# Moving two weight pools to the other side of SBUF, keeping the row-sum reciprocals on chip, and reusing the FFN's operand tiles in the down stage

## The chip, the cores and the metric

The kernel runs on one core of one Trainium2 chip. The metric is the device time of one execution in microseconds; lower is better. Engines are named as in the profile: PE is TensorE (PEld its weight loads), DVE VectorE, ACT ScalarE, POOL GpSimd, SP the engine that issues most of the transfers (SPq its queue).

## What is computed

One layer of a decoder trunk on 1024 tokens plus 16 meta tokens, width 1024, in fp32. Cut to what matters here:

```python
u = rmsnorm(h, attn_norm_w)
# 4 delta-rule heads -> o_gdn (512 columns); 8 softmax heads of width 64 -> o_fox (512 columns)
p = softmax(where(causal, scores, MASK)); o_fox = p @ v
h = h + concat([o_gdn, o_fox]) @ w_out
u2 = rmsnorm(h, ffn_norm_w)
h = h + (silu(u2 @ w_gate) * (u2 @ w_up)) @ w_down      # hidden width 2816
return rmsnorm(h, final_norm_w)[:, 16:]
```

## The kernel before

**Precision.** Every large product is made of three fp32r matmuls: a `split` (L156 to L159) makes a high part by a cast on ACT and a low part by a subtraction on DVE, and high times high, high times low and low times high are accumulated.

**Order of work.** The stages follow each other: input projection, delta rule, attention, out-projection, gate and up stage of the FFN, down stage. On PE the order is the program's, by hand (`manual_schedule`); in attention it comes from a small planner (`PeOrder`) with estimated due times. The other engines' and the queues' orders come from the scheduler of the framework, which puts an instruction where its own timeline says that it will be ready; once emitted, each engine and each queue runs in order.

**Attention** (to L1037). For each of the 8 heads the unnormalised output goes to a DRAM tensor `o_d` in two halves (high and low value parts), and the reciprocals of the row sums are transposed on PE (`prr`, L1034), copied out of PSUM and stored in a DRAM tensor `ri_d` by `att_sums`.

**Out-projection.** The delta-rule half is `wout_gdn` (L1062): 16 units of 12 matmuls, of which six (`RES`) run after attention. Then the softmax half runs over eight token tiles in the order 0, 4, 1, 5, 2, 3, 6, 7. For one tile, `prep` (L1129) loads both halves of `o_d` (`of`) and the reciprocals, spread over the partitions, from `ri_d` (`rb`, one buffer, two transfers, L1137), adds and multiplies on POOL (L1139, L1140), splits into `oh` and `ol` and loads the running sum (`hst`). `out_fox` (L1146) makes 12 matmuls for each half of the columns, adds `hst` on DVE (L1152) and, after the second half, normalises: squares on ACT, a power on POOL (L204), one long DVE instruction (`xn`, L1045). `u_blocks` (L1161) transposes `xn` on PE (`u2t`, 8 transposes) and builds the operands of seven block products `p1` to `p7` (a Strassen-like scheme with 7 instead of 8 products): two of them for tiles 0 to 3, five for tiles 4 to 7. `prep` runs two tiles ahead, `u_blocks` two behind. The tiles of this stage lie in pool `wo1`, on the left side of SBUF over space that the delta-rule half still uses.

**Gate and up stage.** For each of 11 column blocks `j`, `ffn_in` runs 14 units of 12 matmuls (products p1, p6, p2, p7, p5, p4, p3, each for gate and up). `w_ops` loads and combines the weights and splits them into 8 pairs of buffers that rotate; raw weights have four rotating buffers, also used by `down_sums`, which combines the down weights on POOL and stores them in `wt_d`. `act_sums` stores the combined activations in `ao_d`. For `j` = 0 three units (`p1` gate, `p1` up, `p2` gate) have their weights early.

**Down stage.** For each of seven products, `down_ops` (L1347) loads activations and weights in three chunks of 4, 4 and 3 blocks into a new pool `f2`, which is opened after the pools of the stage before are closed, and splits them; 12 matmuls per block and token group follow (L1380).

Of the kernel before, what the change touches and what calls it, by code (L numbers as in the profile page):

```python
# [15 lines left out]
P = 128  # L16
# [21 lines left out]
RES = 6  # L38
WARM = 24
# [55 lines left out]
def tile_hymba_layer(ctx, tc, x, meta, attn_norm_w, w_in, conv_w, a_log, dt_bias, gdn_norm_w,  # L95
# [40 lines left out]
    nc.gpsimd.memset(mhalf, -0.5)  # L136

# [12 lines left out]
    ri_d = dram.tile([FH, S], F32, name="ri_d")  # L150
# [943 lines left out]
    atc.close()  # L1094
# [11 lines left out]
    uoc, pfc, woc, f1c = ExitStack(), ExitStack(), ExitStack(), ExitStack()  # L1106
    uop = uoc.enter_context(tc.tile_pool(name="uop", bufs=1, side="right", reuse_waits="tile"))
    uo = {p: tuple(uop.tile([P, 4, H], F32R, name=f"u{c}_{p}") for c in "hl") for p in ORD}
    pfp = pfc.enter_context(tc.tile_pool(name="pf", bufs=1, side="right", reuse_waits="tile"))
    wo = woc.enter_context(tc.tile_pool(name="wo1", bufs=1, reuse_waits="tile"))  # L1110
    nwb2 = wo.tile([P, D], F32, name="nwb2")
    xns = {}
    turn = {}

    def wo_tile(tag, shape, bufs, nm, dt=F32):
        turn[tag] = turn.get(tag, -1) + 1
        return wo.tile(shape, dt, tag=f"{tag}_{turn[tag] % bufs}", name=f"{tag}_{nm}")

    sq = [P, 4, P]
    for tag, shape, dt in ([(f"br{g}_{i}", sq, F32) for g in range(2) for i in range(2)]  # L1120
                           + [(f"xn2_{i}", [P, D], F32) for i in range(2)] + [(f"ub{i}_0", sq, F32) for i in range(3)]
                           + [(f"hst_{i}", [P, D], F32) for i in range(2)] + [("gap", [P, 808], F32), ("ol_1", sq, F32R),
                              ("ol_0", sq, F32R), ("oh_0", sq, F32R), ("oh_1", sq, F32R), ("of_0", [P, 8, P], F32),
                              ("of_1", [P, 8, P], F32), ("rb_0", sq, F32)]):
        wo.tile(shape, dt, tag=tag, name=f"lay_{tag}")

    pre_u = {}

    def prep(tt, q):  # L1129
        cols = slice(P * tt, P * tt + P)  # L1130
        ht = wo_tile("hst", [P, D], 2, tt)
        oh, ol = (wo_tile(t, [P, 4, P], 2, tt, F32R) for t in ("oh", "ol"))
        of = wo_tile("of", [P, 8, P], 2, tt)
        rb = wo_tile("rb", [P, 4, P], 1, tt)
        q.dma_start(of, o_d[:, :, :, cols].rearrange("i k p c -> p (i k) c"))
        for i in range(2):
            q.dma_start(rb[DH * i:DH * i + DH],  # L1137
                              ri_d[:, cols].rearrange("(m i) c -> i m c", i=2)[i].partition_broadcast(DH))
        G.tensor_tensor(of[:, 0:4], of[:, 0:4], of[:, 4:8], op=ALU.add)  # L1139
        G.tensor_tensor(of[:, 0:4], of[:, 0:4], rb, op=ALU.mult)  # L1140
        cast = split(oh, ol, of[:, 0:4])
        nc.sync.dma_start(ht, h_d[tt])
        pre_u[tt] = (oh, ol, ht)
        return cast

    def out_fox(tt, nb):  # L1146
        oh, ol, ht = pre_u[tt]
        wv = wfs[nb]
        acc = ps_mm(f"wof_{tt}_{nb}")
        mm3(acc, [(oh[:, k], ol[:, k], wv[0][k], wv[1][k]) for k in range(4)])  # L1150
        hb = ht[:, H * nb:H * nb + H]
        V.tensor_add(hb, acc, hb)  # L1152
        if nb:
            xn = wo_tile("xn2", [P, D], 2, tt)
            norm2(ht, nwb2, xn, wo, f"f{tt}")
            nc.sync.dma_start(h_d[tt], ht)
            xns[tt] = xn
# [3 lines left out]
    def u_blocks(tt):  # L1161
# [14 lines left out]
        if tt < 4:  # L1176
            br = [wo_tile(f"br{g}", [P, 4, P], 2, tt) for g in range(2)]
# [29 lines left out]
    def w_ops(v, j, m):  # L1207
        r0, r1 = (f1[0].tile([P, D], F32, tag="raw", bufs=4, name=f"raw_{m}{j}_{i}") for i in range(2))
        for r, f in ((r0, j), (r1, j + NF)):
            w_raw(r, v, f)  # L1210
        a11, a12, a21, a22 = r0[:, :H], r0[:, H:], r1[:, :H], r1[:, H:]
        s2, s3, s4 = (f1[0].tile([P, H], F32, tag=f"ws{i}", bufs=2, name=f"ws{i}_{m}{j}") for i in range(3))
        V.tensor_tensor(s3, a11, a21, op=ALU.subtract)  # L1213
        V.tensor_tensor(a21, a21, a22, op=ALU.add)
        V.tensor_tensor(s2, a21, a11, op=ALU.subtract)
        V.tensor_tensor(s4, a12, s2, op=ALU.subtract)
        for p, src in zip(ORD, (a11, s2, a12, s3, a21, a22, s4)):
            if p not in wops[m, j]:
                w_split(m, j, p, src, f1[0], 8)
            yield  # L1220
# [9 lines left out]
    def down_sums(j):  # L1230
# [9 lines left out]
        for p, t in (("p7", t3), ("p5", b12), ("p6", b22), ("p4", b21)):  # L1240
            nc.sync.dma_start(wt_d[p][:, j], t)
# [12 lines left out]
    def ffn_evict(m, j, p, b):  # L1254
        if (m, j) not in sbs:
            sbs[m, j] = {c: f1[0].tile([P, H], F32, tag=f"{m}{c}", bufs=2, name=f"{m}{c}_{j}")
                         for c in ("xyzw" if m == "g" else "xyz")}
# [17 lines left out]
    def act_sums(j):  # L1275
# [7 lines left out]
        for p, t in zip(ORD, (a11, s2, a12, s3, a21, a22, s4)):  # L1283
            nc.sync.dma_start(ao_d[p][:, j], t)
# [12 lines left out]
    with tc.manual_schedule(engines={mybir.EngineType.PE}):  # L1297
        order = (0, 4, 1, 5, 2, 3, 6, 7)
        cast = prep(order[0], nc.scalar)
        nc.sync.dma_start(nwb2, ffn_norm_w[0].partition_broadcast(P))  # L1300
        prep(order[1], nc.scalar)
        with tc.issue_after(cast.ins):
            wfs.append(wout_block(4, 1))
        early = []
        for i, tt in enumerate(order):
            out_fox(tt, 0)
            if i >= 2:
                u_blocks(order[i - 2])
            out_fox(tt, 1)
            if i + 2 < NT:  # L1310
                prep(order[i + 2], nc.sync)
            if i == 3:
                for m, v in (("g", w_g_v), ("u", w_u_v)):
                    r = wraw.tile([P, WMAX], F32, tag="raw", name=f"raw_{m}")[:, :D]
                    w_raw(r, v, 0)
                    for p, src in (("p1", r[:, :H]), ("p2", r[:, H:]))[:2 if m == "g" else 1]:
                        w_split(m, 0, p, src, pfp, 3)
        u_blocks(order[6])
        done = [("p1", "g"), ("p1", "u"), ("p2", "g")]
        early = [(p, m, ffn_bank(m, 0, p)) for p, m in done[:2]]  # L1320
        u_blocks(order[7])
# [5 lines left out]
        for g in gens.values():
            next(g)
        for p, m, b in early:
            ffn_evict(m, 0, p, b)  # L1330
        ffn_evict("g", 0, "p2", ffn_bank("g", 0, "p2"))
# [3 lines left out]
        f1c.close()  # L1335
        pfc.close()
        uoc.close()

        f2 = ctx.enter_context(tc.tile_pool(name="f2", bufs=1, side="right", reuse_waits="tile"))
        f3 = ctx.enter_context(tc.tile_pool(name="f3", bufs=1, reuse_waits="tile"))  # L1340
# [27 lines left out]
        ops = down_ops(PH2[0])  # L1368
        hs = [f3.tile([P, D], F32, name=f"hs{t}") for t in range(NT)]
# [52 lines left out]
        for n, p in enumerate(PH2):  # L1422
# [46 lines left out]
```

## Time and profile before

| | us |
|---|---|
| median of 3 runs | 1378.21 (1377.46 to 1381.68) |
| the profiled execution's own time | 1382.61 |
| span of its trace | 1380.9 |
| PE busy | 1317.5 (95% of the span) |
| DVE, ACT, POOL busy | 861.8, 545.3, 428.6 |
| mean granted PE clock | 0.976 of full speed |

The trace is of one execution, and its start is 0. A matmul's duration contains pipelined overlap with the next one, so the pace of PE is read from start to start. "Idle before" is the time in which the engine waited just ahead of an instruction, with the work that released it. In a table of stretches, the columns after the stretch are its length, then busy time of PE, PEld, DVE, ACT and POOL with the number of instructions, the granted PE clock, the share of the DMA engines and GB/s. Attention ends near 617 us, the softmax half of the out-projection lies from 638 to 717 us, the gate and up stage ends at 1147.6 us.

### The profile page before, as it was taken

The page shows a single profiled execution, that of the slowest core. Times are in us where ns is not written, and L with a number is a line of the kernel's source. Part 1 is how long each engine was busy: PE and PEld are TensorE (multiplying, and loading weights), DVE is VectorE, ACT ScalarE, POOL GpSimd, SP SyncE. Part 2 cuts the span into 40 slices and gives each one's busy share as a digit, 9 for nine tenths or more (in the row PEclk, how much of TensorE's full clock was granted, in tenths as well). Part 3 has the DMA queues.
Part 4 walks back from the last instruction along what each step waited for, and adds up shares of the span by engine and source line. Part 5 has one row for each costly group of instructions (what it writes and reads, how often), then busy time and mean ns, then how long its engine had stood idle before and what let it go on. Part 6 is the DMA issues. An engine that isn't in the chain of part 4 may idle for free.

```text
span 1380.9 us, 20172 instructions
## 1 busy us (share of the span) xinstructions
PE 1317.5 (95%) x7393; PEld 1141.9 (83%) x7393; DVE 861.8 (62%) x1505; ACT 545.3 (39%) x914; POOL 428.6 (31%) x422
## 2 busy tenths in 40 slices
PE   8999999899999899997778999999999997999997
PEld 8999998899999788875566888888888885888886
DVE  6565779657346588972578666676666645445653
ACT  6443553222233477871354333323323223433341
POOL 3111213211112266731443444433334443020300
PEclk9999999999999999998989999999999998999999
DMA  8131554784397898926665554454554538854542
GB/s 286 64 92 51 146 174 147 211 221 139 128 311 229 215 252 233 231 56 193 189 183 151 176 162 153 144 158 150 164 168 147 159 115 316 338 197 169 213 150 92
DMA packets 200682, 244.25 MB, mean 177 GB/s; under 512 B 19264, under 2 KB 151288, under 8 KB 196744
## 3 DMA queue, kind: packets, MB, share of 16 engines
q1 hardware_dynamic: 197416, 241.40, 56.0%
q10 hardware_dynamic: 3168, 1.57, 0.6%
q8 instruction: 58, 0.95, 0.3%
q14 instruction: 40, 0.33, 0.1%
HBM read 163.72 MB, written 79.21 MB: 176 GB/s over the span
## 4 chain that ended last, share of the span: by engine, by line
PE 72%; DMA 11%; DVE 8%; issue 4%; POOL 2%; SPq 2%; ACT 1%; DVEq 0%; POOLq 0%; ACTq 0%
PE xp L1380 8%; PE yp L1380 6%; PE gd L1227 4%; PE ud L1227 4%; PE ub L1227 4%; PE gb L1227 4%; PE ua L1227 4%; PE ga L1227 4%; DMA rb<-ri_d 3%; PE pj_fk L198 3%; PE pj_fq L198 3%; PE wog L198 3%; PE pt L960 2%; PE ue L1227 2%; PE ge L1227 2%
## 5 line engine op out<-in xcount | busy, mean ns | idle before, releaser
L158 DVE TENSOR_TENSOR al_p<-ra_p,ah_p 128x2048 fp32r<-128x2048 f32 (+1 forms) x21 | 47.0, 2238 | 79.0 <-ACT ah_p L157 79.0
L913 POOL TENSOR_TENSOR bi<-ccol,cr 128x144 f32<-128x144 f32 (+7 forms) x60 | 70.6, 1182 | 57.9 <-DVE sm L929 50.4
L157 ACT CAST ah_p<-ra_p 128x2048 fp32r<-128x2048 f32 (+1 forms) x21 | 37.1, 1768 | 101.7 <-PE yp L1380 50.5
L1380 PE MATMUL xp<-wh_p,ah_p 128*128 128x512 f32 x176 | 70.4, 400 | 6.9 <-ACT wh_p L157 6.9
L1380 PE MATMUL xp<-wl_p,ah_p 128*128 128x512 f32 x176 | 70.5, 400 | 4.4 <-DVE wl_p L158 2.6
L1380 PE MATMUL xp<-wh_p,al_p 128*128 128x512 f32 x176 | 70.2, 399 | 0.0
L1273 POOL TENSOR_TENSOR gz<-gz,uz 128x512 f32<-128x512 f32 x11 | 18.4, 1670 | 164.7 <-ACT wh_u_p L157 127.3
L934 ACT ACTIVATE pr<-pr,sm 128x144 f32<-128x144 f32 (+3 forms) x64 | 50.6, 791 | 16.1 <-DVE sm L929 14.7
L157 ACT CAST wh_u_p<-raw_u 128x512 fp32r<-128x512 f32 x44 | 27.2, 618 | 69.9 <-PE ub L1227 27.5
L158 DVE TENSOR_TENSOR wl_u_p<-raw_u,wh_u_p 128x512 fp32r<-128x512 f32 x44 | 42.7, 970 | 19.3 <-ACT wh_u_p L157 19.3
L158 DVE TENSOR_TENSOR wl_g_p<-raw_g,wh_g_p 128x512 fp32r<-128x512 f32 x44 | 43.5, 990 | 17.5 <-ACT wh_g_p L157 17.4
L158 DVE TENSOR_TENSOR wl_p<-rw_p,wh_p 128x2048 fp32r<-128x2048 f32 (+1 forms) x21 | 47.5, 2262 | 10.7 <-ACT wh_p L157 10.7
L158 DVE TENSOR_TENSOR pl<-pt,ph 128x512 fp32r<-128x512 f32 (+1 forms) x96 | 51.5, 551 | 4.0 <-ACT ph L157 3.5
L157 ACT CAST ph<-pt 128x512 fp32r<-128x512 f32 (+1 forms) x96 | 45.2, 473 | 20.9 <-PE pt L960 19.7
L1380 PE MATMUL yp<-wh_p,ah_p 128*128 128x512 f32 x132 | 51.3, 389 | 0.0
L1380 PE MATMUL yp<-wl_p,ah_p 128*128 128x512 f32 x132 | 51.3, 389 | 0.0
L1380 PE MATMUL yp<-wh_p,al_p 128*128 128x512 f32 x132 | 51.3, 389 | 0.0
L157 ACT CAST wh_g_p<-raw_g 128x512 fp32r<-128x512 f32 x44 | 27.2, 621 | 57.8 <-PE gb L1227 32.6
L960 PE MATMUL pt<-ident,pr 128*128 128x128 f32 x288 | 48.2, 276 | 0.0
L1213 DVE TENSOR_TENSOR ws_g<-raw_g,raw_g 128x512 f32<-128x512 f32 x11 | 8.9, 811 | 61.8 <-DMA raw_g<-in_w_gate_dram 61.8
L1380 PEld LDWEIGHTS xp<-wh_p,ah_p 128*128 128x128 f32 x176 | 34.1, 194 | 14.6 <-ACT wh_p L157 7.3
L926 PE MATMUL sc<-kk,sa 128*128 128x144 f32 (+6 forms) x112 | 41.0, 367 | 4.0 <-issue 3.4
(591 smaller groups left out, 4531.1 us busy)
## 6 DMA issues: line engine op xcount, KB each, us to landing
ra_p<-ao_p SPq DMA_DIRECT2D x14, 1024.0 KB
raw_g<-in_w_gate_dram SPq DMA_DIRECT2D x23, 512.0 KB, 4.3
raw_u<-in_w_up_dram SPq DMA_DIRECT2D x23, 512.0 KB, 5.7
raw_d<-in_w_down_dram SPq DMA_DIRECT2D x22, 512.0 KB, 3.6
wt_p<-raw_d SPq DMA_DIRECT2D x33, 256.0 KB, 2.2
kk<-k_d SPq DMA_DIRECT2D x16, 520.0 KB, 10.1
rw_p<-wt_p SPq DMA_DIRECT2D x8, 1024.0 KB, 6.8
rw_p<-in_w_down_dram SPq DMA_DIRECT2D x6, 1024.0 KB
```

The lines of the kernel that those rows point to most:

```text
L157: cast = nc.scalar.copy(dst_hi, src)
L158: nc.vector.tensor_sub(dst_lo, src, dst_hi.bitcast(F32))
L198: nc.tensor.matmul(dst, a, b, start=first, stop=last)
L913: nc.gpsimd.tensor_tensor(bi[:, :n], ccol[:, h, j:j + 1].broadcast_to([P, n]), cr[:, :n], op=ALU.subtract)
L926: nc.tensor.matmul(sc[:, :b - a], sa[:, q0:q0 + P], kk[:, 0, a:b], start=True, stop=False)
L934: nc.scalar.activation(pr[:, :n], pr[:, :n], AF.Exp, bias=sm[:, np_ - 1:np_], scale=-1.0, accum_out=rsum[:, h, j:j + 1])
L960: nc.tensor.transpose(pt[:rows_k, P * j:P * j + P], pts[j][0][:, c0:c0 + rows_k], ident)
L1213: V.tensor_tensor(s3, a11, a21, op=ALU.subtract)
L1227: nc.tensor.matmul(dst, a[:, c], b[:, k], start=(first and k == 0 and i == 0), stop=(k == 3 and i == 2), skip_group_check=not first)
L1273: G.tensor_tensor(gs[d], gs[d], us[d], op=ALU.mult)
L1380: nc.tensor.matmul(dst, a[:, f, c], b[:, f], start=(first and i == 0 and n == 0), stop=(i == NF - 1 and n == 2), skip_group_check=cont)
```

## The change

- The pools `wraw` and `wsp` (raw and split weights) go from the left to the right side of SBUF. Pool `wo1` goes to the right too and is opened right after attention, over attention's tiles; the FFN's `f1` goes to the right over `wo1`, and the block operands `uop` to the left.
- `att_sums` only takes the reciprocals, into an on-chip tile `rinv`. `ri_d`, its stores, the `rb` loads and the POOL multiply go. In their place `row_scale` copies the tile's reciprocals on POOL, spread to 128 x 512 (`rx`, in the slot `ub0_0` that `u_blocks` also uses), transposes them four times on PE, and DVE multiplies with the result in PSUM.
- The first two tiles are prepared after 26 steps of the delta-rule half that runs after attention. The tile order becomes 0, 4, 1, 5, 2, 6, 3, 7, and `u_blocks` of the last tile but one moves between the two halves of the last `out_fox`.
- In the gate and up stage `p2` of `j` = 0 has its weights early for both gate and up and runs first; the split weights rotate over 7 pairs instead of 8.
- `ao_d` and `wt_d` become one DRAM tensor for each product and chunk. The first three chunks of the down stage are loaded into the space of `p1`'s operands, and split operands go to the spaces of the other products' operands, by explicit tags; `down_ops` for the first product comes before the closing of the pools.

```diff
+ORDER = (0, 4, 1, 5, 2, 6, 3, 7)
...
+    rinv = const.tile([P, FH, NT], F32, name="rinv")
...
-    wraw = wrc.enter_context(tc.tile_pool(name="wraw", bufs=2))
-    wsp = wrc.enter_context(tc.tile_pool(name="wsp", bufs=4))
+    wraw = wrc.enter_context(tc.tile_pool(name="wraw", bufs=2, side="right"))
+    wsp = wrc.enter_context(tc.tile_pool(name="wsp", bufs=4, side="right"))
...
     def att_sums(h):
-        rr = ap2.tile([P, NT], F32, tag="rr", bufs=2, name=f"rr_{h}")
-        V.reciprocal(rr, rsum[:, h])
+        V.reciprocal(rinv[:, h], rsum[:, h])
         yield od.t + 1.0
-        pt = ps_t(f"prr_{h}")
-        nc.tensor.transpose(pt[:NT, :P], rr, ident)
-        rt = ap2.tile([NT, P], F32, tag="rt", bufs=1, name=f"rt_{h}")
-        V.tensor_copy(rt, pt[:NT, :P])
-        nc.sync.dma_start(ri_d[h].rearrange("(j c) -> j c", c=P), rt)
...
+    atc.close()
+    G = nc.gpsimd
+    wo2 = woc.enter_context(tc.tile_pool(name="wo1", bufs=1, side="right", reuse_waits="tile"))
...
+    def row_scale(tt):
+        rx = wo_tile("rx", [P, 4, P], 1, tt, slot="ub0_0")
+        G.tensor_copy(rx.rearrange("p m (i c) -> p (m i) c", i=2), rinv[:, :, tt:tt + 1].broadcast_to([P, FH, DH]))
+        pt = ps_s(f"rbt_{tt}").rearrange("p (a b) -> p a b", a=4)
+        for m in range(4):
+            nc.tensor.transpose(pt[:, m], rx[:, m], ident)
+        rbk[tt] = pt
+
+    def prep(tt):
...
+        nc.sync.dma_start(of, o_d[:, :, :, cols].rearrange("i k p c -> p (i k) c"))
+        G.tensor_tensor(of[:, 0:4], of[:, 0:4], of[:, 4:8], op=ALU.add)
+        row_scale(tt)
+        V.tensor_mul(of[:, 0:4], rbk[tt], of[:, 0:4])
+        cast = split(oh, ol, of[:, 0:4])
...
+    for _ in range(26):
+        od.step_fill()
+    casts = [prep(tt) for tt in ORDER[:2]]
     while od.step_fill():
         pass
...
-                w_split(m, j, p, src, f1[0], 8)
+                w_split(m, j, p, src, f1[0], 7)
...
         if done:
-            units = [x for x in units if x not in done]
+            units = [("p2", "g"), ("p2", "u")] + [x for x in units if x not in done and x[0] != "p2"]
...
+        SETS = (("p6", "p2"), ("p7", "p5"), ("p4", "p3"))
...
-                ra, rw = (f2.tile([P, 4, H], F32, tag=f"r{c}{i}", name=f"r{c}_{p}{f0}") for c in "aw")
-                nc.sync.dma_start(ra[:, :n], ao_d[p][:, f0:f0 + n])
+                if k < len(CH) or k % 3 == 0:
+                    ra, rw = (blk(c, "p1", f"r{x}_{p}{f0}").bitcast(F32) for c, x in ("ha", "lw"))
+                else:
+                    ra, rw = (raws[0].tile([P, 4, H], F32, tag=f"r{x}{k % 3}", name=f"r{x}_{p}{f0}") for x in "aw")
+                nc.sync.dma_start(ra[:, :n], ao_c[p, f0])
...
         ops = down_ops(PH2[0])
+        f1c.close()
+        pfc.close()
```

## Rows read from the trace of the kernel before

**Rows 1.** The page, part 1: PE's busy time and instructions.
```profile
PE 1317.5 (95%) x7393; PEld 1141.9 (83%) x7393; DVE 861.8 (62%) x1505; ACT 545.3 (39%) x914; POOL 428.6 (31%) x422
```

**Rows 2.** Table of stretches, out-projection and start of the down stage.
```profile
617.00:634.15 17.15, 17.12 (x73) 13.45 (x73) 3.46 (x5) 0.58 (x1) 1.29 (x1) 1.00 0.48 141
...
638.35:716.70 78.35, 61.38 (x244) 45.76 (x244) 45.77 (x62) 29.43 (x53) 30.56 (x27) 0.87 0.62 184
716.70:735.65 18.95, 11.74 (x48) 9.00 (x48) 16.58 (x22) 11.65 (x21) 10.46 (x7) 0.82 0.57 143
...
1147.60:1157.83 10.23, 0.79 (x1) 0.29 (x1) 6.72 (x4) 5.70 (x3) 9.11 (x5) 0.60 1.01 381
1157.83:1165.00 7.17, 7.17 (x20) 5.71 (x21) 5.43 (x2) 2.81 (x2) 1.08 (x1) 0.62 0.93 326
```

**Rows 3.** What PE waited for, 600 to 760 us (total us, times, longest).
```profile
PE wof L188 <- ACT oh L157: 9.9, 6, 4.2
PE u2t L1168 <- DVE xn L1045: 9.2, 4, 7.0
PE ga L1227 <- ACT gx L1260: 4.8, 1, 4.8
```

**Rows 4.** Chain that ended last, 676 to 694 us (start, us, what).
```profile
685.49 5.70 DMA rb<-ri_d
...
691.35 1.28 POOL of L1140
```

**Rows 5.** What PE waited for, 1130 us to the end.
```profile
PE xp L1380 <- ACT wh_p L157: 6.9, 1, 6.9
PE xp L1380 <- DVE wl_p L158: 2.6, 1, 2.6
```

**Rows 6.** Chain that ended last, 1141 to 1158 us.
```profile
1144.83 0.25 SPq L1352
...
1145.16 7.32 DMA rw_p<-in_w_down_dram
...
1152.51 1.91 ACT wh_p L157
...
1154.44 3.35 DVE wl_p L158
```

**Rows 7.** Timeline of PE, 697 to 760 us (start, us, instruction).
```profile
705.94 1.03 PE L1168 MATMUL u2t<-ident,xn 128*128 128x128 f32 x8
706.73 0.48 PE L188 MATMUL wof<-whi_wo,oh 128*128 128x512 f32 x1
...
712.42 1.03 PE L1168 MATMUL u2t<-ident,xn 128*128 128x128 f32 x8
```

**Rows 8.** Timeline, 600 to 645 us: the last reciprocal's transpose and POOL's first add.
```profile
612.77 0.27 PE L1034 MATMUL prr<-ident,rr 128*8 128x128 f32 x1
...
625.31 1.29 POOL L1139 TENSOR_TENSOR of<-of 128x512 f32<-128x512 f32 x1 [22.50 <-DMA h_d<-ht]
```

**Rows 9.** Groups on POOL, whole span (count, busy us, mean ns, idle before).
```profile
L1140 POOL TENSOR_TENSOR of<-of,rb 128x512 f32<-128x512 f32 x8 | 10.2, 1277 | 36.3 <-DMA rb<-ri_d 36.3
...
L520 POOL MEMSET up<- 128x512 f32 x2 | 1.1, 526 | 0.2 <-DMA rk_d<-rkt 0.2
```

**Rows 10.** Groups on DVE, 636 to 735.6 us.
```profile
L1045 DVE SCALAR_TENSOR_TENSOR xn<-hst,st_f,nwb 128x1024 f32<-128x1024 f32 x8 | 13.3, 1661 | 5.8 <-POOL st_f L204 5.8
...
L1174 DVE TENSOR_TENSOR ul_p<-ub,uh_p 128x512 fp32r<-128x512 f32 x8 | 8.3, 1033 | 0.7 <-ACT uh_p L1173 0.7
L1174 DVE TENSOR_TENSOR ul_p<-u2t,uh_p 128x512 fp32r<-128x512 f32 x12 | 7.8, 678 | 0.0
L158 DVE TENSOR_TENSOR ol<-of,oh 128x512 fp32r<-128x512 f32 x8 | 7.6, 956 | 26.1 <-ACT oh L157 26.1
```

**Rows 11.** Timeline of DVE, 870 to 912 us: weights for a later block.
```profile
900.02 0.69 DVE L1213 TENSOR_TENSOR ws_g<-raw_g,raw_g 128x512 f32<-128x512 f32 x1 [6.84 <-DMA raw_g<-in_w_gate_dram]
...
902.14 0.69 DVE L158 TENSOR_TENSOR wl_g_p<-ws_g,wh_g_p 128x512 fp32r<-128x512 f32 x1
```

**Rows 12.** Chain that ended last, whole span: one unit of the gate stage.
```profile
913.61 2.72 PE gd L1227 x12
```

More of the change, by code (lines that the diff above doesn't have):

```diff
@@ L1085, in tile_hymba_layer, with wo_tile, load_h @@
         pass
+    atc.close()
+    G = nc.gpsimd
+    woc = ExitStack()
+    wo2 = woc.enter_context(tc.tile_pool(name="wo1", bufs=1, side="right", reuse_waits="tile"))
+    turn, rbk, pre_u = {}, {}, {}
+    def wo_tile(tag, shape, bufs, nm, dt=F32, slot=None):
+        turn[tag] = turn.get(tag, -1) + 1
+        return wo2.tile(shape, dt, tag=slot or f"{tag}_{turn[tag] % bufs}", name=f"{tag}_{nm}")
+    def row_scale(tt):
[6 more added lines that the diff above has]
+    def prep(tt):
+        cols = slice(P * tt, P * tt + P)
+        oh, ol = (wo_tile(t, [P, 4, P], 2, tt, F32R) for t in ("oh", "ol"))
+        of = wo_tile("of", [P, 8, P], 2, tt)
+        nc.sync.dma_start(of, o_d[:, :, :, cols].rearrange("i k p c -> p (i k) c"))
[3 more added lines that the diff above has]
+        cast = split(oh, ol, of[:, 0:4])
+        pre_u[tt] = (oh, ol)
+        return cast
+    def load_h(tt):
+        ht = wo_tile("hst", [P, D], 2, tt)
+        nc.sync.dma_start(ht, h_d[tt])
+        pre_u[tt] += (ht,)
+    nwb2 = wo2.tile([P, D], F32, name="nwb2")
+    nc.sync.dma_start(nwb2, ffn_norm_w[0].partition_broadcast(P))
     od.fill = wout_gdn_all(tiles[len(tiles) - RES:])
     wfs = [wout_block(4, 0)]
+    for _ in range(26):
+        od.step_fill()
+    casts = [prep(tt) for tt in ORDER[:2]]
     while od.step_fill():
@@ L1103, in tile_hymba_layer @@
+    ao_c, ao_d = chunked("ao", ORD)
+    wt_c, wt_d = chunked("wt", ("p5", "p6", "p7", "p4"))
     w_g_v = w_gate.rearrange("(k p) n -> p k n", p=P)
     w_u_v = w_up.rearrange("(k p) n -> p k n", p=P)
[L1106 to L1109, printed above, removed]
@@ L1127, in tile_hymba_layer @@
[L1127 to L1144, printed above, removed]
+    uoc, pfc, f1c = ExitStack(), ExitStack(), ExitStack()
@@ L1146, in out_fox, with blk @@
+    uop = uoc.enter_context(tc.tile_pool(name="uop", bufs=1, reuse_waits="tile"))
+    uop.tile([P, 120], F32, name="upad")
+    def blk(c, p, nm=None):
+        return uop.tile([P, 4, H], F32R, tag=f"u{c}_{p}", name=nm or f"u{c}_{p}")
+    uo = {p: tuple(blk(c, p) for c in "hl") for p in ORD}
+    pfp = pfc.enter_context(tc.tile_pool(name="pf", bufs=1, reuse_waits="tile"))
+    xns = {}
     def out_fox(tt, nb):
@@ L1154, in out_fox @@
             xn = wo_tile("xn2", [P, D], 2, tt)
[L1155 removed]
+            norm2(ht, nwb2, xn, wo2, f"f{tt}")
             nc.sync.dma_start(h_d[tt], ht)
@@ L1176, in u_blocks @@
         if tt < 4:
-            br = [wo_tile(f"br{g}", [P, 4, P], 2, tt) for g in range(2)]
+            br = [wo_tile(f"br{g}", [P, 4, P], 1, tt) for g in range(2)]
             for g, p in enumerate(("p1", "p2")):
@@ L1254, in ffn_evict @@
     def ffn_evict(m, j, p, b):
-        if (m, j) not in sbs:
-            sbs[m, j] = {c: f1[0].tile([P, H], F32, tag=f"{m}{c}", bufs=2, name=f"{m}{c}_{j}")
-                         for c in ("xyzw" if m == "g" else "xyz")}
+        sbs.setdefault((m, j), {})
+        if p in ("p6", "p2"):
+            for c in "xyzw" if m == "g" else "xyz":
+                if c not in sbs[m, j]:
+                    sbs[m, j][c] = f1[0].tile([P, H], F32, tag=f"{m}{c}", bufs=2, name=f"{m}{c}_{j}")
+        elif p == "p1" and not sbs[m, j]:
+            sbs[m, j]["x"] = f1[0].tile([P, H], F32, tag=f"{m}x", bufs=2, name=f"{m}x_{j}")
         t, gs, us = sbs[m, j], sbs["g", j], sbs.get(("u", j))
@@ L1297, in tile_hymba_layer @@
     with tc.manual_schedule(engines={mybir.EngineType.PE}):
[L1298 to L1302, printed above, removed]
+        for tt in ORDER[:2]:
+            load_h(tt)
+        with tc.issue_after(casts[0].ins):
             wfs.append(wout_block(4, 1))
-        early = []
-        for i, tt in enumerate(order):
+        for i, tt in enumerate(ORDER):
             out_fox(tt, 0)
             if i >= 2:
-                u_blocks(order[i - 2])
+                u_blocks(ORDER[i - 2])
+            if i == NT - 1:
+                u_blocks(ORDER[i - 1])
             out_fox(tt, 1)
             if i + 2 < NT:
-                prep(order[i + 2], nc.sync)
+                prep(ORDER[i + 2])
+                load_h(ORDER[i + 2])
             if i == 3:
@@ L1315, in tile_hymba_layer @@
                     w_raw(r, v, 0)
[L1316 to L1321, printed above, removed]
+                    for p, src in (("p1", r[:, :H]), ("p2", r[:, H:])):
+                        w_split(m, 0, p, src, pfp, 4)
+        done = [("p1", "g"), ("p1", "u")]
+        for p, m in done:
+            sbs[m, 0] = {"x": pfp.tile([P, H], F32, name=f"{m}x0")}
+            ffn_evict(m, 0, p, ffn_bank(m, 0, p))
+        u_blocks(ORDER[7])
         woc.close()
         wrc.close()
-        f1[0] = f1c.enter_context(tc.tile_pool(name="f1", bufs=1, reuse_waits="tile"))
-        f1[0].tile([P, 56], F32, name="pad")
-        gens = {m: w_ops(v, 0, m) for m, v in (("g", w_g_v), ("u", w_u_v))}
[L1327 to L1331, printed above, removed]
+        f1[0] = f1c.enter_context(tc.tile_pool(name="f1", bufs=1, side="right", reuse_waits="tile"))
+        f1[0].tile([P, 64], F32, name="pad")
+        f1[0].tile([P, D], F32, tag="raw", bufs=4, name="lay_raw")
+        for c in "hl":
+            f1[0].tile([P, H], F32R, tag=f"w{c}", bufs=7, name=f"lay_w{c}")
+        gens = {m: w_ops(v, 0, m) for m, v in (("g", w_g_v), ("u", w_u_v))}
         for j in range(NF):
@@ L1334, in tile_hymba_layer @@
             down_sums(j)
[L1335 to L1340, printed above, removed]
         lo_, hi_ = slice(0, H), slice(H, D)
         wd_src = {"p1": (0, lo_), "p2": (NF, lo_), "p3": (NF, hi_)}
-        CH = ((0, 4), (4, 4), (8, 3))
+        SETS = (("p6", "p2"), ("p7", "p5"), ("p4", "p3"))
+        raws = [None]
         cnt = [0]
@@ L1368, in tile_hymba_layer @@
         ops = down_ops(PH2[0])
+        f1c.close()
+        pfc.close()
+        f3 = ctx.enter_context(tc.tile_pool(name="f3", bufs=1, side="right", reuse_waits="tile"))
+        raws[0] = f3
         hs = [f3.tile([P, D], F32, name=f"hs{t}") for t in range(NT)]
```

35 lines of the change are left out of this document (11 added, 24 removed).

## The prediction

> **What bounds the kernel now.** I began with the page: PE is busy 1317.5 of 1380.9 us [rows 1], so what can be won without removing matmuls is about 63 us of idle PE and what a lowered clock costs. The next view, the waits of PE, says where the idle time is. Between 600 and 760 us PE waits 9.9 us for `oh`, 9.2 us for `xn` and 4.8 us for one `gx` [rows 3]; after 1130 us it waits 9.5 us for the first down weights [rows 5]. The table of stretches gives the same places their length: in the softmax half of the out-projection PE is busy 61.4 of 78.4 us at a clock of 0.87, in the 19 us after it 11.7 at 0.82, and ahead of the down stage almost nothing for 10.2 us [rows 2]. In the gate and up stage units follow each other at 2.72 us without a gap [rows 12].
>
> The chain of waits says why. From 639 to 699 us it repeats one period, once for each tile: the `rb` transfer (5.7 us here), then POOL's multiply (1.28 us), after which the single `rb` buffer may be loaded again [rows 4]. POOL waited 36.3 us for `rb` over eight tiles [rows 9]. Ahead of the down stage the chain is the weight load from 1145.16 us (7.32 us), a cast (1.91) and a subtraction (3.35), in a row [rows 6]: the load was issued only when the gate stage was ending.
>
> **The change part by part: out-projection.** *Removed:* the `rb` loads, and with them the period of rows 4. What is late next is the work itself, so I add it up for PE and for DVE from the first `out_fox` to the first `p6` gate unit (735.65 us before, the end of a stretch in rows 2).
>
> PE: 24 matmuls take from 706.73 to 712.42 us, 0.237 each, and eight transposes 0.79, 0.10 each [rows 7]. So 192 matmuls are 45.5, 64 `u2t` transposes 6.4, 24 of the new transposes (six tiles; two come earlier) 2.4, and four units of 2.72 [rows 12] 10.9: 65.2 us.
>
> DVE: it was busy 45.8 + 16.6 = 62.4 us in the two stretches [rows 2]. The new multiply has one input in PSUM; the nearest row is the subtraction from `u2t` at 0.678 [rows 10], eight are 5.4. One more weight split comes early (0.7), and two tiles' multiply and `ol` (2 x (0.68 + 0.96) = 3.3) [rows 10] come before the stretch. Sum 65.2 us: by accident the same as PE. In the last 19 us, where nothing waited for `rb`, DVE was busy 16.58 of 18.95, 87.5% [rows 2]. At that share 65.2 us of work need 74.5.
>
> Two things are added to it. First, DVE instructions with both inputs in SBUF were longer than their neighbours beside POOL's work: `ul` from `ub` 1.03 against 0.678 from PSUM [rows 10]. Over the 16 `xn` and `ul` of that kind and the `ol` the excess is some 8 us in 97; with POOL as busy in a shorter stretch I put 2 us more, 0 to 5. The Trainium skill's page "SBUF — State Buffer", section "Who interferes with whom", has a rule that speaks against this change: a DVE instruction with two SBUF inputs and a GpSimd instruction that reads SBUF exclude each other for their whole length. The trace agrees in kind with that pair of rows, and no run here yet shows the pair under the new copy.
>
> Second, PE's order now contains the new transposes, which wait for POOL's copy `rx`. For tiles 6 and 7 `rx` shares a slot with `b12` of `u_blocks`, so the path is three DVE instructions (3 x 0.68), then the copy, against 12 matmuls (2.84) of cover. No row shows such a copy. Below it is bounded by a memset of the same size, 0.53, above by the multiply it replaces, 1.28 [rows 9]; I take 1.28, the same shape and place. The path is then 3.3 plus hand-offs and whatever POOL has ahead: 1.5 us of wait, twice, 3 us in all (0 to 8). The Trainium skill's "GPSIMD Engine Reference", section 4.1, has two-input work about twice slower and one-input work near line rate; by that the copy would be an estimated 0.64 and the two waits together 1.3 us shorter.
>
> *Start.* Today the first `out_fox` starts at 638.35, 4.2 us after the delta-rule half ends at 634.15 [rows 2]. With `wo1` over attention's tiles the first two tiles are prepared under that half. Added there: eight transposes, 0.8 us. The second tile's copy must follow the first tile's transposes in the one `rx` slot, and no PE work lies between them: 1.28 plus hand-off, 1.5 us. If POOL's queue has the copy behind its first add, which could not start before 625.31 [rows 8], PE (there after 24 matmuls, 617.06 + 5.6 = 622.7) waits some 5 us more. I take the short case: start at 634.15 + 0.8 + 1.5 = 636.5.
>
> Together 636.5 + 74.5 + 2 + 3 = 716.0 against 735.65, and one more unit (2.72) is then done: **22.4 us**. The bound from above is PE's own work alone, 636.5 + 65.2: 36.7 us. The clock losses of that stretch are inside both, since the durations I add are those at full rate.
>
> *Queues.* SP loses 16 stores and loads of reciprocals (ACT's queue the four of the first tiles) and takes over the two first `of` loads. A store behind which they could stand waits for one delta-rule tile, 12 x 0.237 = 2.8 us; the remaining matmuls cover it.
>
> **Attention.** Eight `prr` transposes leave PE's path [rows 8]; at 0.10 each **0.8 us**. Eight copies on DVE and eight stores go too; PE hardly waited for either, so nothing more. The side of `wraw` and `wsp` shifts all left pools by the same amount as the right ones, so I cost the earlier stages at nothing, plus or minus 2.
>
> **Down stage.** Chunk 0 now goes into `p1`'s operands, which PE leaves 12 units before the end, 33 us, and reads a tensor that was complete many blocks earlier. Load, two casts and two subtractions of a chunk were 7.3 + 1.9 + 3.4 us and one more pair [rows 6]; chunk 1 has the same slots after it, and its 10.9 us of matmuls cover chunk 2. If so, the 10.2 us of idle PE go, and the 7.17 us at 0.62 clock [rows 2], which cost 7.17 x 0.38 = 2.7. I take **11.5** of the 12.9, the rest for a wait behind the gate stage's own ACT and DVE work. The ends are 12.9 and 0: nothing, if the loads stay late.
>
> **Gate and up stage.** Seven pairs instead of eight delay a split by up to one unit, 2.72 us. The split at 902.14 us [rows 11] is for the unit at 913.61 [rows 12]: 11 us of lead hide it, and the sum has nothing for it.
>
> **Sum.** 22.4 + 0.8 + 11.5 = 34.7. The profiled execution took 1382.6 us, so 1347.9 for it; that execution is 4.4 us above the median of the three runs, 1378.2, and against the median the same gain gives **1343.5**.
>
> **The rivals.**
> 1. *The copy takes the place of the load.* In-order PE waits in each tile for POOL's copy behind adds, powers and `u_blocks`' POOL work, and the period stays near nine us. For it: POOL was busy 41 of the 97 us [rows 2]. Against it: six of the eight copies depend on nothing late. The gain is then about 9 at both ends of the stage (1.9 at the start, 4.8 for `gx` [rows 3], and clock), 9 + 0.8 + 11.5 = 21: 1357. Chance 0.20.
> 2. *The loads stay late.* SP's queue is in order; if the scheduler leaves the first chunk behind the last stores, as now [rows 6], the change does not do what it says in this stage. 22.4 + 0.8 + 1 = 24: 1354. Chance 0.13.
> 3. *PE alone sets the end.* DVE's backlog is absorbed in the gate stage: 36.7 + 0.8 + 12.9 = 50: 1328. Chance 0.12.
> 4. *Slower: the gate and up stage loses its lead.* The raw weights' load already ends DVE's idle time there (6.84 us [rows 11]). With seven pairs and new addresses the four raw buffers come free later. It decides from the point where the load lands more than 11 us later; at 5 us lost in each of ten blocks, 50 - 34.7 = 15 slower: 1393. Against it: one unit is 2.72 us. Chance 0.05.
>
> **How the numbers follow.** My case has 0.47, and 0.03 is for a gain eaten up by reordered queues. What a measurement of this kernel can tell from no change is about 0.3%, 4 us. Faster by more: 0.92; within: 0.03; slower: 0.05. The range reaches from 1330, which leaves out part of rival 3, to 1364, which holds rivals 1 and 2 and the long end of the start.
>
> **What would show it.** Right: no transfer in the chain between 640 and 700 us; PE's waits for `oh` gone; the first `p6` gate unit near 716 us; PE idle under 2 us ahead of the down stage; the first chunk's loads issued some 20 us or more before the gate stage ends. Wrong: waits of the `rbt` transposes for `rx` of over 8 us in all (rival 1), a first down load next to the last gate unit (rival 2), or units of the gate stage with gaps (rival 4).

## The result and the profile after

| | before | after |
|---|---|---|
| median | 1379.54 (4 runs) | 1361.32 (4 runs, 1359.36 to 1362.23) |
| the profiled execution's own time | 1382.61 | 1361.58 |
| span of its trace | 1380.9 | 1359.8 |
| PE busy | 1317.5 | 1308.9 (96%) |
| mean granted PE clock | 0.976 | 0.986 |

The ratio is 0.9866 (95% interval 0.9845 to 0.9887): 18.2 us faster. The forecast was 34.7 us faster, in a range from 14 to 48. By stage, from the two traces (attention ends where the first `wog` follows the last matmul `po`; then come the first `p6` gate unit, the end of the last gate or up unit, and the place from which the down stage's matmuls run on, its second matmul before and its first after; then the end):

| stage | before | after | gained | forecast |
|---|---|---|---|---|
| start to end of attention | 617.06 | 610.46 | 6.6 | 0.8 |
| out-projection, to the first `p6` unit | 118.59 | 110.19, with one more unit of 2.72 | 11.1 | 22.4 |
| gate and up stage | 411.95, 151 units | 419.09, 150 units | -9.9 | 0 |
| PE all but idle ahead of the down stage | 10.23 | 0 | 10.2 | down stage: |
| down stage to the end | 223.07 | 220.06 | 3.0 | 11.5 for both |

The sum is 21.0, the difference of the two spans (21.1). The profiled execution of before lay 3.1 us over its median and that of after 0.3 over its own, which leaves the 18.2.

The waits of PE, which answer to [rows 3] (600 to 760 us), then 735 to 1150 us, then 1100 us to the end, which answers to [rows 5] (total us, times, longest):

```profile
PE rbt L1096 <- POOL rx L1093: 15.1, 3, 9.3
PE gb L1237 <- ACT wh_g_p L158: 3.6, 1, 3.6
PE u2t L1178 <- DVE xn L1040: 1.8, 2, 1.2
PE wof L189 <- ACT oh L158: 0.9, 1, 0.9
...
PE gd L1237 <- DVE gz L1282: 4.9, 6, 1.8
...
PE xp L1395 <- DVE wl_p L159: 1.8, 1, 1.8
```

The waits for `oh`, `xn` and `gx`, 23.9 us in [rows 3], are down to 2.7. A new one stands in their place, 15.1 us for `rx`, the copied reciprocals, and two smaller ones: 3.6 for the first `p6` weight and 4.9 for `gz` in the gate stage. The table of stretches, which answers to [rows 2] (the stretches are cut at the stages of this kernel):

```profile
628.86:720.65 91.79, 70.23 (x330) 56.23 (x328) 64.28 (x88) 40.33 (x72) 32.06 (x29) 0.93 0.49 154
...
720.65:730.00 9.35, 8.80 (x25) 6.53 (x26) 8.80 (x14) 3.88 (x8) 1.68 (x2) 0.64 0.41 131
...
1139.74:1147.00 7.26, 7.26 (x33) 6.01 (x33) 4.32 (x5) 3.58 (x4) 3.76 (x3) 1.00 0.80 282
```

From the first `out_fox` to the first `p6` unit PE is busy 70.2 of 91.8 us and DVE 64.3. The gate stage now begins with 9.35 us at a granted clock of 0.64, after the wait of 3.6. The down stage begins at full rate where before it had 10.23 us of idle PE and 7.17 us at 0.62 [rows 2]. The chain that ended last, around its start (start, us, what), which answers to [rows 6]:

```profile
1134.14 2.88 PE gd L1237 x12
1137.02 2.72 PE ud L1237 x12
1139.74 29.92 PE xp L1395 x132
```

No transfer and no split stands between the last unit and the first `xp`. The timeline of SP shows why: the first chunk's loads go out 29 us ahead of it.

```profile
1110.76 0.39 SPq L1369 DMA_DIRECT2D rw_p<-in_w_down_dram  x1
1111.24 0.52 SPq L1363 DMA_DIRECT2D ra_p<-ao_p  x1
```

**Where the 15.1 us come from.** 14.3 of them lie at tiles 6 and 7, the two whose copy must wait for a block tile of `u_blocks`; the other 0.8 lie at the second tile, ahead of the first `out_fox`. The timeline of PE at tile 6 (start, us, instruction; in brackets the idle time ahead and what ended it), of DVE and of POOL:

```profile
653.01 0.66 PE L1178 MATMUL u2t<-ident,xn 128*128 128x128 f32 x4 [0.37 <-ACT br L1190]
...
656.05 0.39 PE L191 MATMUL wof<-whi_wo,ol 128*128 128x512 f32 x1
665.71 1.12 PE L1096 MATMUL rbt<-ident,rx 128*128 128x128 f32 x4 [9.27 <-POOL rx L1093]
...
686.42 1.11 PE L1096 MATMUL rbt<-ident,rx 128*128 128x128 f32 x4 [5.07 <-POOL rx L1093]
...
656.01 1.28 DVE L1040 SCALAR_TENSOR_TENSOR xn<-hst,st_f,nwb 128x1024 f32<-128x1024 f32 x1
657.21 0.68 DVE L1162 TENSOR_TENSOR hst<-wof,hst 128x512 f32<-128x512 f32 x1
657.80 0.68 DVE L1195 TENSOR_TENSOR br<-u2t,br 128x512 f32<-128x512 f32 x1
...
659.20 0.69 DVE L1199 TENSOR_TENSOR ub<-u2t,ub 128x512 f32<-128x512 f32 x1
...
666.20 2.29 DVE L1040 SCALAR_TENSOR_TENSOR xn<-hst,st_f,nwb 128x1024 f32<-128x1024 f32 x1 [3.37 <-POOL st_f L205]
...
660.51 1.71 POOL L1104 TENSOR_TENSOR of<-of 128x512 f32<-128x512 f32 x1 [4.77 <-DVE hst L1162]
662.18 1.71 POOL L1201 TENSOR_TENSOR br<-br,ub 128x512 f32<-128x512 f32 x1
663.85 1.26 POOL L1184 TENSOR_TENSOR ul_p<-br,uh_p 128x512 fp32r<-128x512 f32 x1
665.05 0.60 POOL L1093 COPY rx<-rinv 128x512 f32<-128x512 f32 x1
...
667.36 1.60 POOL L1093 COPY rx<-rinv 128x512 f32<-128x512 f32 x1
```

The transposes `u2t` end at about 653.4, and after the 12 matmuls that follow PE has nothing to do from 656.44 us (656.05 + 0.39) on. Three things make the wait of 9.27:

- *DVE's queue.* The three subtractions of `u_blocks` take 2.1 us, as forecast, but begin only at 657.80: the other tiles' `ol`, `xn` and `hst` stand ahead of them. The last one, at 659.20, is the last reader of `b12` in slot `ub0_0` and ends at 659.89, 3.45 us after PE ran out of work.
- *POOL's queue.* From then on the slot is free, but three instructions stand ahead of the copy, the next tile's add and two of `u_blocks`: 4.54 us, with 0.62 ahead of them in which that add is not ready either.
- *The copy itself:* 0.60, and the hand-off.

At tile 7 the same path costs 5.07 us.

### The profile page after: what moved, and what is told of

It reads as the page before. It is cut to its first block, busy times and chain, and to the rows that moved or that the text cites. A ratio compares the mean times of both kernels' runs of the same rounds, so it can differ in the third digit from the quotient of the medians.

```text
span 1359.8 us, 20162 instructions
## 1 busy us (share of the span) xinstructions
PE 1308.9 (96%) x7417; PEld 1137.2 (84%) x7417; DVE 859.9 (63%) x1505; ACT 543.6 (40%) x914; POOL 424.0 (31%) x422
## 4 chain that ended last, share of the span: by engine, by line
PE 56%; DMA 15%; DVE 14%; POOL 7%; issue 5%; SPq 1%; ACT 1%; DVEq 0%; POOLq 0%; ACTq 0%
PE xp L1395 8%; PE yp L1395 6%; DMA raw_u<-in_w_up_dram 5%; PE pj_fk L199 3%; PE pj_fq L199 3%; DMA wt_p<-raw_d 3%; DMA raw_d<-in_w_down_dram 2%; PE wog L199 2%; PE pt L961 2%; DVE wl_u_p L159 2%; PE po L982 1%; PE pj_k L190 1%; PE pj_k L189 1%; PE pj_v L191 1%; PE pj_q L191 1%
## 5 line engine op out<-in xcount | busy, mean ns | idle before, releaser
L159 DVE TENSOR_TENSOR wl_u_p<-raw_u,wh_u_p 128x512 fp32r<-128x512 f32 x44 | 47.0, 1069 | 15.4 <-ACT wh_u_p L158 15.4
L159 DVE TENSOR_TENSOR wl_g_p<-raw_g,wh_g_p 128x512 fp32r<-128x512 f32 x44 | 38.7, 881 | 23.4 <-ACT wh_g_p L158 23.4
L930 DVE CUSTOM_DVE_ANT_0 pr<-sc,bi 128x144 f32<-128x144 f32 (+3 forms) x64 | 31.5, 492 | 15.7 <-PE sc L928 11.8
```

The costliest lines, as they stand in the source:

```text
L159: nc.vector.tensor_sub(dst_lo, src, dst_hi.bitcast(F32))
L930: V.tensor_tensor_reduce(out=pr[:, a:b], in0=sc[:, :b - a], in1=bi[:, a:b], scale=1.0, scalar=3e38 if i == 0 else sm[:, i - 1:i], op0=ALU. ...
```

## The experiments

The profiled runs' waits and stretches are read at the same places as above. Ratios are against the kernel before, with their 95% interval; "the change" is the kernel after it (1361.32 us, 0.9866).

**Is it the slot? (e1)** The middle tile of `u_blocks` goes where the third one goes anyway, and the copy has slot `ub0_0` to itself.

```diff
-        b12, t2, t3 = (wo_tile(f"ub{i}", [P, 4, P], 1, tt) for i in range(3))
+        t2, t3 = (wo_tile(f"ub{i}", [P, 4, P], 1, tt) for i in (1, 2))
+        b12 = t3
```

> Only b12 of u_blocks moves, into the tile that its one reader t3 overwrites, so the copied reciprocals rx have a slot of their own. Slot theory: the 15.1 us that PE waits for rx are held by the shared slot; they fall under 5 us, the lowered clock beside them mostly goes, and the kernel takes about 1350 us. Rival (POOL's queue is the limit): PE's waits for rx move to other tiles, stay over 10 us in all, and the time stays within 4 us of the changed kernel's 1361.

Measured: 1353.25 us, ratio 0.9814 (0.9795 to 0.9833), 8.1 us less than the change. PE's waits from 605 to 760 us, and the same copy on POOL's timeline:

```profile
PE u2t L1178 <- DVE xn L1040: 3.9, 2, 2.9
PE gb L1238 <- ACT wh_g_p L158: 3.6, 1, 3.6
PE rbt L1096 <- POOL rx L1093: 3.5, 2, 2.7
...
657.53 1.29 POOL L1104 TENSOR_TENSOR of<-of 128x512 f32<-128x512 f32 x1 [4.22 <-DMA of<-o_d]
658.75 0.62 POOL L1093 COPY rx<-rinv 128x512 f32<-128x512 f32 x1
```

The copy now stands right behind the add of its tile and ahead of the work of `u_blocks`. The wait falls from 15.1 to 3.5 us, 2.1 come back as waits for `xn`, and the stretch from the first `out_fox` to the first `p6` unit from 91.79 to 81.22 us (632.61 to 713.83). It was the slot, and by it POOL's order; copying itself is not dear.

**Is it the eighth pair? (e2, e3)** e2 has eight pairs of split weights. Their space comes from the scratch tile `dt` of `down_sums`, which e2 does without; e3 is the control, seven pairs without that tile.

```diff
-                w_split(m, j, p, src, f1[0], 7)
+                w_split(m, j, p, src, f1[0], 8)
...
-        t3 = f1[0].tile([P, H], F32, tag="dt3", bufs=1, name=f"dt3_{j}")
-        G.tensor_tensor(t3, b22, b12, op=ALU.subtract)
-        G.tensor_tensor(b12, b12, b11, op=ALU.subtract)
-        G.tensor_tensor(b22, b22, b12, op=ALU.subtract)
+        G.tensor_tensor(b11, b12, b11, op=ALU.subtract)
+        G.tensor_tensor(b12, b22, b12, op=ALU.subtract)
+        G.tensor_tensor(b22, b22, b11, op=ALU.subtract)
```

(The stores name the tiles accordingly, and the lines that lay out the pool have eight pairs too; e3 has the edit of `down_sums` alone.)

> Eight pairs of split weights again in the gate and up stage; the room comes from down_sums working without its scratch tile. Theory (one pair less costs the lead): PE's waits for gz in that stage, 4.9 us in six pieces, go, and the time is about 5 us less, 1356. Rival (the stage merely starts with its raw weights late): the gz waits stay near 5 us and the time within 2 us of 1361.

> The control of the run with eight pairs: down_sums without its scratch tile, seven pairs as in the changed kernel. Both theories: gz waits near 5 us, time within 2 us of 1361. If it is as fast as the run with eight pairs, the scratch tile and not the pairs is what mattered.

Measured: e2 1356.48 us, 0.9841 (0.9823 to 0.9859); e3 1359.89 us, 0.9855 (0.983 to 0.988). In e2 PE waits for nothing between 735 and 1150 us; in e3 this is left:

```profile
PE gd L1237 <- DVE gz L1281: 1.8, 2, 1.3
```

From the first `p6` unit to the start of the first `xp` the change took 418.9 us (the table's 419.1 count to the end of the last unit), e3 416.5, e2 414.4 (150 units without a gap are 408.0). In the medians it is 4.8 us for both edits together. All runs of e2 (1355.70 to 1358.24) lie below all runs of the change (1359.36 to 1362.23), and e9 below stands to e1 in the same way, 4.2 us less. So the missing pair and the scratch tile together cost 4 to 5 us. What each of them costs is not shown: the runs of e3 (1356.10 to 1361.48) overlap those of both. Single traces do not settle it either. That of e6 below, which has seven pairs and the scratch tile, takes 413.5 us from the first `p6` unit to the first `xp`, after a stretch from the first `out_fox` that is 3.8 us longer than the change's, and has this left of the wait:

```profile
PE gd L1238 <- DVE gz L1283: 0.7, 2, 0.5
```

**What holds the first `p6` weight? (e4, e7, e8, e9)** Its wait of 3.6 us, with the low clock behind it, is some 7 us. In the change the raw weights are loaded late, behind the last store of `h_d` on SP's queue. e4 puts that store on ACT's queue; e7 does so too, and puts the tiles of `wo1` in another order, which was to lay the raw weights over tiles that are free early (its lines are those of e8 below, with `ub0_0` ahead of them and a filler tile behind).

```diff
-            nc.sync.dma_start(h_d[tt], ht)
+            (nc.scalar if tt == ORDER[-1] else nc.sync).dma_start(h_d[tt], ht)
```

> The last tile's store of the running sum goes to ACT's queue, so the raw weights of the first block no longer stand behind it in SP's queue. Late-start theory: the raw loads issue before 700 us instead of at 710, PE's wait of 3.6 us ahead of the first p6 unit and the low clock after it (3 us) go, the gz waits get smaller too, and the time is 1351 to 1355. Rival (one pair less costs the lead): the p6 wait goes, the gz waits stay, 1355 to 1357.

> The changed kernel with the tiles of pool wo1 laid out in another order, so that the first block's raw weights land on the split and raw attention tiles that are free early and not on the norm weights and on b12, and the last tile's store on ACT's queue. Theory (the overlay holds the raw loads, the store ahead of them in SP's queue next): the raw loads issue 5 to 8 us earlier than at 710 to 714 us, PE's wait of 3.6 us ahead of p6 and part of the low clock go, and the time is 1355 to 1358. Rival (DVE's backlog holds the weights, not the loads): the loads are earlier, the wait stays, 1360 to 1365.

Measured: e4 1365.38 us, 0.9904 (0.9886 to 0.9921); e7 1365.63 us, 0.9875 (0.9846 to 0.9904). Both missed: the loads go no earlier with respect to the unit, and the wait is 3.6 and 5.1 us. e4 is slower than the change by 4 us, for a reason that was not looked into; e7 is so in the medians, but its ratio cannot be told from the change's. SP's timeline of e4, whose first `p6` unit comes about as late as that of the change, then what SP waited for from 690 to 725 us, in e4 and in e7:

```profile
712.43 3.27 SPq L1215 DMA_DIRECT2D raw_g<-in_w_gate_dram  x2
...
SPq L1215 <- DVE xn L1040: 14.2, 1, 14.2
...
SPq L1219 <- DVE ub L1203: 17.1, 1, 17.1
```

The store was not what held the load: with it gone from the queue the load waits 14.2 us for `xn`, the last user of tiles that it overlays. In e7 it waits 17.1 us for `ub`, the last reader of `b12`, so that layout did not do what it was meant to do. e8 puts the slot of e1, the pairs of e2, a layout without gap and the store on ACT together; e9 has the slot and the pairs alone.

```diff
+    for tag, shape, dt in ([("oh_0", [P, 4, P], F32R), ("ol_0", [P, 4, P], F32R), ("of_0", [P, 8, P], F32),
+                           ("oh_1", [P, 4, P], F32R), ("ol_1", [P, 4, P], F32R), ("of_1", [P, 8, P], F32)]):
+        wo2.tile(shape, dt, tag=tag, name=f"lay_{tag}")
```

> The slot of its own for the copied reciprocals, eight pairs of split weights, the new layout of wo1 and the last store on ACT's queue together. If the three causes are separate, the gains add: 8 us (slot), 3 to 5 (pairs), 3 to 5 (layout), so 1343 to 1348. If one hides another, 1349 to 1353, no better than the slot alone.

> The changed kernel with two edits only: the copied reciprocals have their slot to themselves, and eight weight pairs without the scratch tile of the down sums; the layout of the out-projection's pool and the queue of the last store are as in the change. Theory (the slot and the pairs are separate losses, and the layout and the store on ACT's queue brought nothing in the version with all edits): about 1348 us, within 3 us of that version, with the slot's waits near 3.5 us, no wait for gz, and the wait for the p6 weight still there, since the weight's combination stands on DVE behind the last block's instructions whenever its load lands. Rival (the early raw loads of the version with all edits were worth something): 1353 us or more, and a p6 wait above 3.6 us.

Measured: e8 1349.18 us, 0.9761 (0.9735 to 0.9786); e9 1349.10 us, 0.9775 (0.9756 to 0.9794). The layout and the store bring nothing that the times show. In e8 the raw load does go out early, 14 us ahead of its first use, and PE's wait does not change:

```profile
696.44 0.38 SPq L1219 DMA_DIRECT2D raw_g<-in_w_gate_dram  x1
...
708.76 0.60 ACT L1280 ACTIVATE gw<-ga 128x512 f32<-128x512 f32 x1
...
709.56 0.69 DVE L1282 TENSOR_TENSOR gw<-ua,gw 128x512 f32<-128x512 f32 x1 [0.82 <-PE ua L1241]
710.17 0.68 DVE L1227 TENSOR_TENSOR ws_g<-raw_g,raw_g 128x512 f32<-128x512 f32 x1
...
712.34 0.62 ACT L158 CAST wh_g_p<-ws_g 128x512 fp32r<-128x512 f32 x1 [2.98 <-DVE ws_g L1229]
713.01 0.79 PE L1241 MATMUL gb<-uh_p,wh_g_p 128*128 128x512 f32 x1 [3.55 <-ACT wh_g_p L158]
```

DVE's queue has the combination of the weights behind `gw`, the product with the result of the `p2` up unit. That unit is the last one that PE has, so when DVE comes to the weights PE already stands, and `gw`, three instructions that combine the weights and a cast, 3.5 us, lie bare. The change has the same order, `gw` at 717.20 us and the first combination at 717.81. Read from these traces, it is the order of DVE's queue; that is not shown by a run, since a version with the combination ahead of `gw` was not run.

**Do the slots decide when the down loads go? (e5, e6)** e5 loads the first three chunks into buffers of the pool that is opened after the gate stage's pools are closed, and calls `down_ops` behind that, as before. e6 makes `ao` and `wt` whole DRAM tensors again and leaves the slots.

```diff
-                if k < len(CH) or k % 3 == 0:
+                if k >= len(CH) and k % 3 == 0:
...
-        ops = down_ops(PH2[0])
         f1c.close()
         pfc.close()
...
+        ops = down_ops(PH2[0])
```

(The three chunks share two pairs of that pool's buffers, `r1` and `r2` of each kind, so the third waits for the first.) And e6:

```diff
-        t = {(p, f0): dram.tile([P, n, H], F32, name=f"{nm}_{p}{f0}") for p in ps for f0, n in CH}
-        return t, {(p, f0 + i): t[p, f0][:, i] for p in ps for f0, n in CH for i in range(n)}
+        w = {p: dram.tile([P, NF, H], F32, name=f"{nm}_{p}") for p in ps}
+        t = {(p, f0): w[p][:, f0:f0 + n] for p in ps for f0, n in CH}
+        return t, {(p, i): w[p][:, i] for p in ps for i in range(NF)}
```

> The changed kernel, but the first three chunks of the down stage are loaded into tiles of the pool that opens after the gate stage's pools are closed, instead of into the space of p1's operands. Theory (where the chunk is loaded decides when): the first loads issue at the end of the gate stage or behind it, PE waits 8 to 12 us there and loses another 2 to 3 at the lower clock, and the time is 1361 + 10 to 15, about 1373. Rival (the split of the DRAM tensors by chunk is what lets the loads go early): the loads still issue early and the time stays near 1361.

> The changed kernel, but each product's activations and weights lie in one DRAM tensor again, with the chunks as slices of it; the slots in SBUF are as changed. Theory (the slots decide): the first chunk's load waits for the last block's store of p1 at most, some 15 us later than now but still some 12 us before the gate stage ends, so that PE waits 0 to 4 us and the time is 1361 to 1365. Rival (the chunked tensors are needed): the loads issue at the end of the stage, PE waits about 10 us, 1373.

Measured: e5 1384.21 us (10 runs), 1.003 (1.0011 to 1.0048); e6 1360.36 us (1352.45 to 1362.8), 0.9833 (0.9795 to 0.987). In e6 the first loads go out at 1109.06 us, as early as in the change, and PE waits for none of them: splitting the tensors was not needed. In e5 (the waits of PE; the chain that ended last; the table of stretches; the last line is the first of the last four stores on SP's timeline of the kernel before):

```profile
PE xp L1395 <- ACT wh_p L158: 17.6, 1, 17.6
...
1153.25 0.32 SPq L1298
...
1153.63 0.42 SPq L1363
...
1154.14 7.20 DMA rw_p<-in_w_down_dram
...
1161.36 1.91 ACT wh_p L158
...
1145.70:1163.30 17.60, 0.04 (x1) 0.00 (x0) 2.99 (x3) 3.79 (x2) 6.31 (x5) 0.61 0.64 244
1163.30:1170.50 7.20, 5.65 (x13) 4.14 (x14) 6.53 (x3) 3.80 (x2) 0.00 (x0) 0.52 1.04 404
...
1151.03 0.32 SPq L1284 DMA_DIRECT2D ao_p<-uy  x1
```

The slots decide, together with the place of the call that goes with them: a buffer of the later pool cannot be loaded by a call ahead of its opening. The change's whole gain is gone. It costs 23 us, more than was expected: the load goes out 8 us after the last unit, behind POOL's `act_sums` and the last stores of `ao_d` that wait for it, and after the wait of 17.6 us PE's first 7.2 us have a granted clock of 0.52. That is later than in the kernel before, where the load went out at 1145.16 us [rows 6], 2.4 us before the last unit ended and ahead of the last four of those stores. So the 23 us are more than what the change's slots gained, to which the table's 13.2 is nearer.

## Why the prediction was off

The sign held and the time lies in the range, but the gain was half of the forecast. By its own steps:

- **The transfers go: right.** No load of reciprocals is left, and the waits for `oh` and `xn` fall from 19.1 to 2.7 us.
- **"3 us in all (0 to 8)" for the copy at tiles 6 and 7: the step that failed.** It was 14.3 there. The place was right, and so was the length of the three DVE instructions (2.1 us); the copy was even shorter than taken (0.60 and 1.07 against 1.28). What was mis-sized is what stands ahead of them: 1.5 us a time was to hold the hand-offs and "whatever POOL has ahead", and at tile 6 DVE was 4.4 us late with its first subtraction (653.4 to 657.80) and POOL's queue took 5.2 more. The change has the slot in common with `b12`, so the copy goes behind `b12`'s reader and whatever the scheduler finds ready by then; e1 takes the slot away, and most of the wait with it. Rival 1 was this at two of eight tiles: its argument against ("six of the eight copies depend on nothing late") held for the six. Its mark, over 8 us of waits for `rx`, is met, though its period of nine us in each tile is not.
- **DVE's share: right but for that wait.** DVE was busy 64.3 us, forecast 65.2. The stretch took 91.79 us against 79.5 (74.5 + 2 + 3), 12.3 more, and 11.3 of it are what the waits for `rx` were over their 3. In e1, where 2.7 of them are left in it, it is 81.22.
- **The start: better than forecast.** First `out_fox` at 628.86, 18.4 us after attention; forecast 636.5 - 617.1 = 19.4. PE waited 0.80 us there for the second tile's copy, priced at 1.5. The short case held, but not because the copy stood ahead of the first add. It stood behind it, and the add ran at 613.00 us, long before the 625.31 of [rows 8]; what held the copy was the first tile's transposes (POOL's timeline):

```profile
613.00 1.29 POOL L1104 TENSOR_TENSOR of<-of 128x512 f32<-128x512 f32 x1 [9.74 <-DMA of<-o_d]
616.63 0.61 POOL L1093 COPY rx<-rinv 128x512 f32<-128x512 f32 x1 [2.34 <-PE rbt L1096]
```

- **Attention, 0.8: measured 6.6, not explained.** Ten traces with the same code up to here have the last `po` between 609.36 and 614.66 us, against 616.90 in the one trace of before. So up to 5 us is what one trace differs from the next, and a gain of 2.2 to 7.5 us is left, of which only the eight `prr` transposes are accounted for.
- **Gate and up stage, nothing: the second step that failed.** "Eleven us of lead" were read at one split of a middle block. The lost 9.9 us are 4.9 for `gz`, 3.4 of low clock (9.35 x 0.36) and 0.6 at the first `p6` unit, and 1 us over. The first term is rival 4 in small, 5 us where it had 50: e2 removes it with the eighth pair and the scratch tile, though which of the two matters is open. The second is the out-projection's: a wait of 3.6 us there is paid a second time behind it.
- **Down stage, 11.5: right,** at 13.2; the wait behind DVE's work that it left room for was 1.8 us. e5 bears out the reason given, the slot, and e6 shows that the split tensors have no part in it. (Rival 2 took the first load of the kernel before to stand behind the last stores; it stood ahead of the last four.)
- **The sum.** With 14.3 in place of 3 and 9.9 in place of 0 the forecast of 34.7 would have been 13.5, and the early stages' surplus (5.8) and the down stage's (1.7) bring it to the 21.0 between the two traces. Without that unexplained surplus the 18.2 us between the medians would be some 12, outside the range: that the time lies in it is in part luck.

The Trainium skill's page "GPSIMD Engine Reference", section 4.1, by which the copy would be an estimated 0.64 us, was the better price than the 1.28 taken: it took 0.60 and 0.62 where DVE ran nothing with two SBUF inputs beside it. The rule of the Trainium skill's page "SBUF — State Buffer", section "Who interferes with whom", is seen at the next copy. On the timeline above it began at 667.36, while DVE's `xn` of two SBUF inputs was running; `xn` ends at 668.49 and the copy at 668.96, 0.47 us later and 1.60 after its start: that fits the two excluding each other, and here it costs nothing, since PE needed that copy only at 674.34. The two other long copies of this trace, 1.10 us at 642.08 and 1.07 at 685.30, end in the same way 0.48 and 0.46 us after a DVE instruction with two SBUF inputs. The price was wrong, then, but it was not what decided: the queue ahead of the copy did.

## What to carry to other kernels

A helper that has to run early must not borrow a slot from work that runs late: the slot's last reader fixes the earliest place of the helper in its queue, and an in-order queue then adds everything that was ready in between. When a load is removed from a path, list, for the instruction that replaces it, what stands ahead of it in its queue, by name and duration, rather than a lump for hand-offs. And a transfer cannot start before its destination is free: slots that an earlier product leaves 12 units before the end let the loads go 29 us ahead of their stage and removed its start-up (13 us), while finer DRAM tensors did nothing; and where the raw weights waited for tiles that they overlay, taking a store out of their queue did nothing.

The best version found is e9: two edits on top of the change, 1349.10 us, 2.25% less than before (interval 2.06 to 2.44) and 12 us less than the change. e8 is no different from it.

## What was not expected of the hardware

A wait of PE was paid twice. After the 9.27 us of idle time at tile 6 the matmuls of the next product start 0.43 us apart, where they start 0.23 apart at full rate; after only 3.56 us of it, ahead of the first `p6` unit, the granted clock over the next 9.35 us was 0.64, so part of them ran at the lower of the two levels, 1.2 GHz, and 3.4 us were lost. The second payment is not the same each time: over the 9.35 us behind the same wait of 3.6 us the granted clock was 0.63 to 0.64 in the change, e2, e4, e5 and e6, 0.70 in e8 and e9, and 0.82 in e1 and e3, a loss of 1.7 to 3.5 us. The matmuls behind the wait of 9.27 us, on PE's timeline:

```profile
667.48 0.63 PE L191 MATMUL wof<-whi_wo,ol 128*128 128x512 f32 x1
667.91 0.63 PE L189 MATMUL wof<-whi_wo,oh 128*128 128x512 f32 x1
...
672.25 0.39 PE L189 MATMUL wof<-whi_wo,oh 128*128 128x512 f32 x1
672.48 0.39 PE L190 MATMUL wof<-wlo_wo,oh 128*128 128x512 f32 x1
```
